# One inference step of a hybrid trunk: every other half linear takes its PSUM bank from the pool of the other products

## The chip, the cores and the metric

The kernel runs on one core of a Trainium2 chip. The metric is the device time of one execution in microseconds (us). The kernel before was timed in three runs: 2755.78, 2758.85 and 2760.88 us, median 2758.85. One execution was profiled; its own time is 2755.11 us and its span, from the first to the last instruction, 2753.0 us. All times below are counted from the start of that span.

## The reference

Two layers with shared weights run over 128 context tokens and 512 latent tokens, with D = 1024. Cut to what the change touches, a layer computes:

```python
h = rms_norm(x, lp['g_pre1']) * (1 + sc1) + sh1
(cb, cc, cx, aq, ak, av, dn_q, dn_k, dn_v, dn_z, dn_beta, dn_a, gate_logits) = jnp.split(h @ lp['w_in'], SPLIT_IDX, axis=-1)
# short convolution, attention and gated DeltaNet give ya, yb, yc
mix = (ga * ya + gb * yb + gc * yc) @ lp['w_o']
x = x + gt1 * rms_norm(mix, lp['g_post1'])
h2 = rms_norm(x, lp['g_pre2']) * (1 + sc2) + sh2
ffn = (jax.nn.silu(h2 @ lp['w_gate']) * (h2 @ lp['w_up'])) @ lp['w_down']
x = x + gt2 * rms_norm(ffn, lp['g_post2'])
```

So at the end of each half of a layer there is a seam: a linear (`w_o` or `w_down`), a norm of its result over all 1024 channels, the residual sum, a second norm over all channels, and then the first linears that read it.

## The kernel before

The activations stand transposed: channels on the 128 partitions, the 640 tokens along the free axis, eight tiles for 1024 channels. The tokens are cut into two halves of 320 columns, called half 0 and half 1. Every weight and activation is split into a high and a low part, and a product is three matmuls (L365, L366, L367: high by high, high by low, low by high). A linear of one block of 128 outputs over 1024 inputs is thus 8 x 3 = 24 matmuls of 128x320 for each half, added up in one PSUM bank.

PSUM has two pools of banks in this kernel. `lbank` (L71) gives the tag `l`, three buffers; it serves the linears alone. `bank` (L74) gives the tag `c`, five buffers; it serves everything else: transposes, attention, DeltaNet, the modulation, and the sums of squares of the norms, where a matmul with a matrix of ones (L157) adds up the channels.

Most linears are written by `linear`, which runs both halves of one weight block together. Near a seam another form is used, in which half 1 runs behind half 0: `group` (L412) and the end of `lin_res` (L465) first run all their blocks for half 0 with `lin_half` (L386), then all for half 1. `lin_res` does so for its last six blocks of `w_o` and `w_down`, `group` for the first linears of the next stage (five in the feed-forward; in a layer's start five, one of them the small `wg` linear, which takes its bank itself).

What is written at a seam, in the order of the program text: six half linears of half 0; then `norm(0)`, which sums the squares (tile `ln`), multiplies and adds the residual (L175 and on), squares and adds up the result again and sums it with a second matmul of ones (tile `pn`, in `half_rstd`, L154); then six half linears of half 1, with the pieces of the next norm's application between them; then `norm(1)` with its own `ln` and `pn`; then the half linears of half 0 of the next stage, then those of half 1. The `pn` of a half is therefore written ahead of the half linears that run while it is being worked out.

A scheduler of the language sets the order on each engine when the program is built. It may put an instruction ahead of others that were written earlier, if its operands and its buffer are there. Buffers of one tag are handed out in the order in which the program asks for them. Each engine then works through its own list in that order, and waits on semaphores for the others.

Of the kernel before, what the change touches and what calls it, by code (L numbers as in the profile page):

```python
# [16 lines left out]
HF = NT // 2  # L17
# [35 lines left out]
def tile_trunk(ctx: ExitStack, tc: tile.TileContext, I: dict, O: list, layers=DEPTH):  # L53
# [17 lines left out]
    def lbank():  # L71
        return pp.tile([P, 512], F32, tag="l", name="l", bufs=NL)

    def bank(name):  # L74
        return pp.tile([P, 512], F32, tag="c", name=name, bufs=NB)
# [4 lines left out]
    def hv(t, h):  # L80
        return t[:, h * HF:(h + 1) * HF]
# [282 lines left out]
    def mm3(out, wh, wl, ah, al, first, last):  # L364
        T.matmul(out, lhsT=wh, rhs=ah, start=first, stop=False)  # L365
        T.matmul(out, lhsT=wh, rhs=al, start=False, stop=False)  # L366
        T.matmul(out, lhsT=wl, rhs=ah, start=False, stop=last)  # L367

    def wblocks(src, nk, keep=None):
# [13 lines left out]
            k += n  # L383
        return out

    def lin_half(blocks, acts, h, ev):  # L386
        pb = lbank()[:, :HF]
        i = 0
        for hi, lo, nk in blocks:
            for j in range(nk):  # L390
                ah, al = acts[i]
                mm3(pb, hi[:, j, :], lo[:, j, :], hv(ah, h), hv(al, h), i == 0, i == len(acts) - 1)
                i += 1
        ev(h, pb)
# [17 lines left out]
    def group(items, side=None):  # L412


        bl = [b if callable(b) or isinstance(b, list) else wblocks(b, len(a), k) for b, a, _, k in items]
        for h in range(2):
            for b, (_, a, ev, _) in zip(bl, items):
                if callable(b):
                    b(h)
                else:  # L420
                    lin_half(b, a, h, ev)
                if h == 0:
                    next(side or iter(()), None)
            drain(side)
# [40 lines left out]
    def lin_res(srcw, acts, ys, gs, keeps, part, after, xe, end=False, side=iter(())):  # L465
# [39 lines left out]
        for h in range(2):  # L505
            for i, b in enumerate(bl):
                lin_half(b, acts, h, ev(n0 + i))
                next(side, None)
            drain(side)
            side = norm(h)  # L510
            next(side, None)
# [914 lines left out]
```

## Time and profile before

| what | value |
| --- | --- |
| median of three runs | 2758.85 us |
| profiled execution, own time | 2755.11 us |
| its span | 2753.0 us |
| PE (TensorE matmuls) busy | 2692.1 us, 98% |
| DVE (VectorE) busy | 1564.1 us, 57% |
| ACT (ScalarE) busy | 1256.7 us, 46% |
| mean granted TensorE clock | 0.994 |
| chain that ended last | PE 84%, DVE 7%, DMA 4%, ACT 3% |

Busy time is the sum of what the engine's instructions took, overlaps counted once. PE's matmuls are pipelined: a 128x320 matmul is shown with some 0.31 us, but the next one starts about 0.147 us behind it. The time between starts is therefore the one to count with. In a timeline row the figures are the start, the length, the engine, line and operation, the tiles as out<-in, the shape and the count of equal ones in a row; in brackets stands the idle time of the engine before it and what ended that.

### The profile page before, as it was taken

To read this page: it belongs to the slowest core of one execution; us is meant where nothing else is said; L and a number is where in the kernel's file an instruction comes from. 1 tells how busy PE (TensorE), PEld (TensorE's weight loads), DVE (VectorE), ACT (ScalarE), POOL (GpSimd) and SP (SyncE) were. 2 spreads that over 40 slices of the span, in tenths; PEclk is the share of its full clock that TensorE was granted. 3 is DMA by queue.
4 is the path that set the end of the run, shared out by engine and by line. 5 is a ranking of instruction groups with operands and counts; after the bars stand their busy time and mean duration, and the time that the engine had idled before them with its cause. 6 is when DMAs were issued, how large, how long until landed. Compare 5 with 4: busy or idle time off the path is not lost.

```text
span 2753.0 us, 49627 instructions
## 1 busy us (share of the span) xinstructions
PE 2692.1 (98%) x19706; PEld 2576.6 (94%) x19706; DVE 1564.1 (57%) x3385; ACT 1256.7 (46%) x2863; POOL 26.8 (1%) x148
## 2 busy tenths in 40 slices
PE   7999999999999999999999999999999999999998
PEld 3899998999899999999989999999999999999997
DVE  5586575477744744224476875754777465432344
ACT  4533554565534633223455345545655364332343
POOL 0000000000000000000000000000000000000001
PEclk9999999999999999999999999999999999999999
DMA  8542355533464344444533323333223532222241
GB/s 243 79 78 55 79 93 105 93 66 97 156 164 153 128 131 153 129 155 146 169 90 71 75 49 85 95 85 87 71 93 120 135 105 72 78 73 73 77 124 56
DMA packets 387800, 288.15 MB, mean 105 GB/s; under 512 B 18699, under 2 KB 348145, under 8 KB 387569
## 3 DMA queue, kind: packets, MB, share of 16 engines
q1 hardware_dynamic: 387568, 285.00, 39.5%
q8 instruction: 154, 2.52, 0.4%
q14 instruction: 78, 0.63, 0.1%
HBM read 251.86 MB, written 33.07 MB: 103 GB/s over the span
## 4 chain that ended last, share of the span: by engine, by line
PE 84%; DVE 7%; DMA 4%; ACT 3%; issue 1%; SPq 0%; POOL 0%; DVEq 0%; ACTq 0%
PE l L365 23%; PE l L366 23%; PE l L367 23%; PE pm L326 1%; DMA wraw<-in_w_in_dram 1%; DMA wm<-in_w_mod_dram 1%; PE ptT L785 1%; DMA rowb<-gd 1%; PE po L795 1%; PE scan L1083 1%; PE po L797 1%; PE sco L365 1%; PE po L796 1%; DVE Tt L1002 1%; PE scan L1091 1%
## 5 line engine op out<-in xcount | busy, mean ns | idle before, releaser
L94 ACT CAST whi<-wraw 128x512 fp32r<-128x512 f32 (+1 forms) x540 | 332.3, 615 | 840.6 <-PE l L366 796.1
L95 DVE TENSOR_TENSOR wlo<-wraw,whi 128x512 fp32r<-128x512 f32 (+1 forms) x540 | 367.1, 681 | 525.7 <-ACT whi L94 512.6
L365 PE MATMUL l<-hh,whi 128*128 128x320 f32 x1856 | 587.0, 316 | 3.1 <-ACT ccs L449 3.1
L366 PE MATMUL l<-hl,whi 128*128 128x320 f32 x1856 | 579.8, 312 | 0.0
L367 PE MATMUL l<-hh,wlo 128*128 128x320 f32 x1856 | 579.3, 312 | 0.0
L365 PE MATMUL l<-h2h,whi 128*128 128x320 f32 x1248 | 387.4, 310 | 0.0
L366 PE MATMUL l<-h2l,whi 128*128 128x320 f32 x1248 | 385.3, 309 | 0.0
L367 PE MATMUL l<-h2h,wlo 128*128 128x320 f32 x1248 | 385.3, 309 | 0.0
L365 PEld LDWEIGHTS l<-hh,whi 128*128 128x128 f32 x1856 | 349.8, 188 | 6.8 <-ACT ccs L449 3.6
L366 PEld LDWEIGHTS l<-hl,whi 128*128 128x128 f32 x1856 | 349.9, 189 | 1.9
L367 PEld LDWEIGHTS l<-hh,wlo 128*128 128x128 f32 x1856 | 349.7, 188 | 1.0
L365 PEld LDWEIGHTS l<-h2h,whi 128*128 128x128 f32 x1248 | 234.6, 188 | 7.0 <-ACT fs L429 3.1
L366 PEld LDWEIGHTS l<-h2l,whi 128*128 128x128 f32 x1248 | 234.7, 188 | 0.0
L367 PEld LDWEIGHTS l<-h2h,wlo 128*128 128x128 f32 x1248 | 234.6, 188 | 0.0
L365 PE MATMUL l<-ah,whi 128*128 128x320 f32 x544 | 169.0, 311 | 0.0
L366 PE MATMUL l<-al,whi 128*128 128x320 f32 x544 | 168.2, 309 | 0.0
L367 PE MATMUL l<-ah,wlo 128*128 128x320 f32 x544 | 168.0, 309 | 0.0
L365 PE MATMUL l<-rsh,whi 128*128 128x320 f32 x384 | 119.7, 315 | 0.0
L366 PE MATMUL l<-rsl,whi 128*128 128x320 f32 x384 | 118.4, 312 | 0.0
L367 PE MATMUL l<-rsh,wlo 128*128 128x320 f32 x384 | 118.2, 309 | 0.0
L365 PEld LDWEIGHTS l<-ah,whi 128*128 128x128 f32 x544 | 102.2, 188 | 2.2 <-issue 1.3
L367 PEld LDWEIGHTS l<-ah,wlo 128*128 128x128 f32 x544 | 102.3, 188 | 0.0
(428 smaller groups left out, 5299.2 us busy)
## 6 DMA issues: line engine op xcount, KB each, us to landing
wraw<-in_w_in_dram SPq DMA_DIRECT2D x256, 256.0 KB, 4.9
wm<-in_w_mod_dram SPq DMA_DIRECT2D x80, 512.0 KB, 4.7
wraw<-in_w_gate_dram SPq DMA_DIRECT2D x88, 256.0 KB, 2.9
wraw<-in_w_up_dram SPq DMA_DIRECT2D x88, 256.0 KB, 3.3
wraw<-in_w_down_dram SPq DMA_DIRECT2D x80, 256.0 KB, 2.9
mixo<-mixd SPq DMA_DIRECT2D x32, 320.0 KB, 5.9
wm<-in_w_mod_dram SPq DMA_DIRECT2D x32, 256.0 KB, 4.7
wraw<-in_w_pb_dram SPq DMA_DIRECT2D x32, 256.0 KB, 2.8
```

What stands on the lines that cost most here:

```text
L94: A.copy(hi, src)
L95: V.tensor_sub(lo, src, hi.bitcast(F32))
L326: T.matmul(pm[32 * u:32 * u + 2, 0:256], lhsT=sc[:, k, :], rhs=w[:, u * 256:(u + 1) * 256], start=(n == 0), stop=(n == KD - 1))
L365: T.matmul(out, lhsT=wh, rhs=ah, start=first, stop=False)
L366: T.matmul(out, lhsT=wh, rhs=al, start=False, stop=False)
L367: T.matmul(out, lhsT=wl, rhs=ah, start=False, stop=last)
L785: T.transpose(pt[:, i, q * P:(q + 1) * P], sm_[q][:, kt * P:(kt + 1) * P], ident)
L795: T.matmul(po, lhsT=vh, rhs=th, start=(kt == 0), stop=False)
L796: T.matmul(po, lhsT=vl, rhs=th, start=False, stop=False)
L797: T.matmul(po, lhsT=vh, rhs=tl, start=False, stop=(kt == 4))
L1002: V.tensor_add(Tt[:, j + 1:32, 0:j], Tt[:, j + 1:32, 0:j], tv)
L1083: T.matmul(pst[:, 1, :], lhsT=XT[h, d][:, c, :], rhs=r, start=True, stop=True)
```

## The change

`lin_half` keeps a turn that flips with every call. Calls one, three, five and so on take a bank of the tag `l` as before; the others take one of the tag `c`, under the name `lc`. Nothing else is changed: all instructions and their shapes are the same, 18,024 matmuls among them.

```diff
@@ -383,8 +383,12 @@
             k += n
         return out
 
+    turn = [0]
+
     def lin_half(blocks, acts, h, ev):
-        pb = lbank()[:, :HF]
+
+        turn[0] ^= 1
+        pb = (lbank() if turn[0] else bank("lc"))[:, :HF]
         i = 0
         for hi, lo, nk in blocks:
             for j in range(nk):
```

The built order moves on PE at the seams. The first place is the seam of `w_o` in layer 0, half 1, from the sum of squares `ln` to the second sum `pn` (the tiles `l` and `lc` are the first linears of the feed-forward for half 0, `ct` is a transpose). Before:

```order
L157 MATMUL ln_10568<-sqt_10544,ones_66 128x320
L366 MATMUL l_10693<-h2l0_9844,wkh_10637 128x320
...
L365 MATMUL l_10726<-h2h0_9843,wkh_10649 128x320
...
L365 MATMUL l_10757<-h2h0_9843,wkh_10661 128x320
...
L365 MATMUL l_10790<-h2h0_9843,wkh_10673 128x320
...
L366 MATMUL l_10790<-h2l6_9856,wkh_10679 128x320
L157 MATMUL pn_10613<-acc_10590,ones_66 128x320
L261 MATMUL ct_10626<-ident_64,rows_10618 128x128
L367 MATMUL l_10790<-h2h6_9855,wkl_10680 128x320
```

The same place on PE in the changed kernel:

```order
L157 MATMUL ln_10568<-sqt_10544,ones_66 128x320
L367 MATMUL l_10693<-h2h3_9849,wkl_10638 128x320
L367 MATMUL l_10757<-h2h0_9843,wkl_10662 128x320
...
L365 MATMUL l_10821<-h2h0_9843,wk_10683 128x320
...
L367 MATMUL l_10821<-h2h7_9857,wk_10684 128x320
L157 MATMUL pn_10613<-acc_10590,ones_66 128x320
L261 MATMUL ct_10626<-ident_64,rows_10618 128x128
L365 MATMUL lc_10726<-h2h0_9843,wkh_10649 128x320
...
L365 MATMUL lc_10790<-h2h0_9843,wkh_10673 128x320
```

The three products of the tag `l` (10693, 10757, 10821) now stand ahead of `pn`, and both products of the tag `c` (10726, 10790) stand behind it. Between the last `ln` matmul and `pn` there were 91 matmuls, and now there are 59.

The second place is the seam of `w_down` in layer 0, half 1, into the first linears of layer 1 (`wg` is the small linear, `l_16025` the first one of half 1, `bgG` belongs to the DeltaNet gates). Before, on PE:

```order
L157 MATMUL ln_15749<-sqt_15725,ones_66 128x320
L366 MATMUL l_15867<-hl4_15050,wkh_15829 128x320
...
L365 MATMUL l_15929<-hh0_15041,wkh_15847 128x320
...
L825 MATMUL l_15960<-hh0_15041,wg_15811 32x320
...
L365 MATMUL l_15982<-hh0_15041,wk_15857 128x320
...
L157 MATMUL pn_15794<-acc_15771,ones_66 128x320
L836 MATMUL bgG_16150<-cst_65,lg_15818 128x16 x2
...
L365 MATMUL l_16025<-hh0_15041,wkh_15823 128x320
```

The same place on PE in the changed kernel:

```order
L157 MATMUL ln_15749<-sqt_15725,ones_66 128x320
L366 MATMUL l_15867<-hl4_15050,wkh_15829 128x320
L366 MATMUL l_15929<-hl2_15046,wkh_15847 128x320
...
L829 MATMUL l_15960<-hl2_15046,wg_15811 32x320
...
L157 MATMUL pn_15794<-acc_15771,ones_66 128x320
L365 MATMUL lc_15898<-hh0_15041,wkh_15835 128x320
...
L365 MATMUL lc_15982<-hh0_15041,wk_15857 128x320
...
L365 MATMUL l_16025<-hh0_15041,wkh_15823 128x320
```

Here 93 matmuls stood between the last `ln` and `pn`, and now 44 do; the 48 of the two `lc` products come behind `pn` and ahead of half 1.

## Rows read from the trace of the kernel before

**Rows 1.** The page's first part: busy us, share and count of PE.

```profile
PE 2692.1 (98%) x19706; PEld 2576.6 (94%) x19706; DVE 1564.1 (57%) x3385; ACT 1256.7 (46%) x2863; POOL 26.8 (1%) x148
```

**Rows 2.** Timeline of PE at the seam of w_o, layer 0: start, us, engine...

```profile
897.02 0.41 PE L365 MATMUL l<-mh,wkh 128*128 128x320 f32 x1 [1.46 <-ACT y L481]
...
902.71 0.41 PE L365 MATMUL l<-mh,wk 128*128 128x320 f32 x1 [1.35 <-ACT y L481]
...
906.34 0.31 PE L365 MATMUL l<-mh,whi 128*128 128x320 f32 x1
...
909.87 0.70 PE L157 MATMUL ln<-acc,ones 128*128 128x320 f32 x2
...
910.56 0.81 PE L157 MATMUL ln<-sqt,ones 128*128 128x320 f32 x2
910.96 0.55 PE L366 MATMUL l<-h2l,wkh 128*128 128x320 f32 x1
911.35 0.30 PE L367 MATMUL l<-h2h,wkl 128*128 128x320 f32 x1
...
922.74 0.42 PE L365 MATMUL l<-h2h,wkh 128*128 128x320 f32 x1 [0.99 <-DVE fg L431]
...
925.79 0.70 PE L157 MATMUL pn<-acc,ones 128*128 128x320 f32 x2
```

**Rows 3.** Timeline of PE at the seam of w_o, layer 1.

```profile
2247.93 0.41 PE L365 MATMUL l<-mh,wkh 128*128 128x320 f32 x1 [1.45 <-ACT y L481]
...
2253.66 0.41 PE L365 MATMUL l<-mh,wk 128*128 128x320 f32 x1 [1.34 <-ACT y L481]
...
2281.09 0.56 PE L365 MATMUL l<-h2h,wkh 128*128 128x320 f32 x2 [0.57 <-ACT h2h L188]
```

**Rows 4.** Timeline of PE at the seam of w_down, layer 0, half 1.

```profile
1436.93 0.81 PE L157 MATMUL pn<-acc,ones 128*128 128x320 f32 x2 [1.45 <-DVE acc L152]
...
1442.24 0.90 PE L365 MATMUL l<-hh,wkh 128*128 128x320 f32 x2 [4.15 <-ACT hh L188]
```

**Rows 5.** Windows, last ln matmul to pn: stretch, length, busy us (count), clock, DMA.

```profile
884.17:898.16 13.99, 12.53 (x82) 12.11 (x82) 11.97 (x28) 8.20 (x19) 0.00 (x0) 1.00 0.20 56
...
910.56:925.79 15.23, 14.24 (x96) 13.82 (x95) 15.08 (x38) 11.59 (x27) 0.00 (x0) 1.00 0.78 276
1391.69:1405.79 14.10, 14.10 (x95) 13.71 (x94) 12.19 (x30) 7.83 (x17) 0.77 (x10) 1.00 0.11 22
...
1420.70:1436.93 16.23, 14.78 (x112) 12.70 (x111) 14.63 (x35) 9.70 (x26) 0.00 (x0) 0.98 0.78 225
2235.09:2249.07 13.98, 12.53 (x83) 12.04 (x82) 11.97 (x28) 8.16 (x18) 0.00 (x0) 1.00 0.20 56
...
2261.50:2277.62 16.12, 16.12 (x108) 15.78 (x107) 16.08 (x41) 11.15 (x27) 0.00 (x0) 1.00 0.59 211
```

**Rows 6.** Timeline of DVE: the last addition before pn, w_o, half 1, both layers.

```profile
925.01 0.48 DVE L152 TENSOR_TENSOR acc<-acc,sqt 128x320 f32<-128x320 f32 x1
...
2276.76 0.49 DVE L152 TENSOR_TENSOR acc<-acc,sqt 128x320 f32<-128x320 f32 x1
```

**Rows 7.** PE past the opening seams: waits for a bank, layers 0 and 1.

```profile
114.53 0.64 PE L365 MATMUL l<-hh,whi 128*128 128x320 f32 x1 [2.75 <-ACT ccs L449]
114.96 0.47 PE L366 MATMUL l<-hl,whi 128*128 128x320 f32 x1
115.23 0.47 PE L367 MATMUL l<-hh,wlo 128*128 128x320 f32 x1
...
1482.67 0.42 PE L365 MATMUL l<-hh,whi 128*128 128x320 f32 x1 [0.33 <-ACT ccs L449]
```

**Rows 8.** Granted clock behind the wait of 4.15 us, and matmuls in it.

```profile
1438.40:1445.20 6.80, 2.96 (x11) 2.93 (x12) 5.04 (x11) 3.81 (x8) 0.00 (x0) 0.50 0.52 102
...
1443.20 0.47 PE L366 MATMUL l<-hl,wkh 128*128 128x320 f32 x1
1443.47 0.47 PE L367 MATMUL l<-hh,wkl 128*128 128x320 f32 x1
```

## The prediction

> **What bounds the kernel now.** I read the page's busy times first, then the gaps of PE in the timeline, then the seams in windows. The page has PE busy for 2692.1 us of a span of 2753.0 us [rows 1]: the kernel is its matmuls, and a change can win only what PE idles or lose by making it idle more. A half linear of 24 matmuls takes 3.53 us from its first start (906.34) to the next instruction's (909.87 [rows 2]), 0.147 us for each. I take this pace to be the same for a bank of either pool, so what counts is how long PE stands at semaphores.
>
> At the seams of `w_o` PE stands for banks: 1.46, 1.35 and 0.99 us in layer 0 [rows 2], 1.45 and 1.34 us in layer 1 [rows 3]. Each is the first matmul of a half linear that waits for the eviction of the linear three before it (ACT `y`, DVE `fg`): three `l` buffers aren't enough there. Together that is 6.6 us. At the seam of `w_down` in layer 0 PE waits 1.45 us at `pn` for the last addition of squares, and then 4.15 us for the first input of half 1 [rows 4]. At the seam of `w_o` in layer 1 it waits 0.57 us for such an input [rows 3].
>
> The third thing to see is how long a `pn` takes to become ready. From the second `ln` matmul of a half to its `pn` the six stretches last 13.99, 15.23, 14.10, 16.23, 13.98 and 16.12 us [rows 5]. DVE is busy for 11.97 to 16.08 us of them, so this chain (multiply, add the residual, square, add up, eight times) goes at the pace of DVE and ACT and not of PE. That PE could come to `pn` at 925.79 without a gap [rows 2], and be busy for all of 14.10 and 16.12 us in two of the stretches [rows 5], is because its list had enough other matmuls to fill them.
>
> **The change, part by part.** No instruction is added, taken away or resized; 42 half linears change their bank, and the built order moves around them. DVE, ACT and SP move a few rows at the same places, with the same instructions; I cost that at nothing, because what they do there is paced by the same chain, and put its doubt into the range.
>
> *The bank waits that go.* Half linears now rotate over three `l` and up to five `c` buffers. The five waits above are at linears that get a buffer earlier: -6.6 us, and no less than 0.
>
> *The place of `pn`.* The order shows a cost. `pn` itself takes a `c` buffer, and is asked for ahead of the half linears that used to run while it ripened. As an `lc` product gets a `c` buffer only after `pn` has got its own, all `lc` products stand behind `pn` on PE, and only every other product is left ahead of it. PE takes its list in order: at 1436.93 it stood 1.45 us at `pn` [rows 4] with products of the other half behind it. So PE now arrives at `pn` early, and waits there, with the `lc` matmuls queued behind. In the changed order the matmuls between the second `ln` and `pn` are 72 and 59 (`w_o`, layer 0, half 0 and half 1), 68 and 44 (`w_down`, layer 0), 72 and 44 (`w_o`, layer 1). At 0.147 us they take 10.58, 8.67, 10.00, 6.47, 10.58 and 6.47 us. The `ln` itself takes 0.65 us of PE (910.56 to 911.35, less one matmul in between [rows 2]). I take the chain to be as long as before, but to end where `pn` could have begun: the last addition ended at 925.01 + 0.48 = 925.49 and 2276.76 + 0.49 = 2277.25 [rows 6], some 0.25 and 0.32 us ahead of `pn` with the time to start. Chain less matmuls less `ln` gives the new waits:
>
> - `w_o`, layer 0: 13.99 - 10.58 - 0.65 = 2.8, and 15.23 - 0.25 - 8.67 - 0.65 = 5.7 us
> - `w_down`, layer 0: 14.10 - 10.00 - 0.65 = 3.5, and 16.23 - 6.47 - 0.65 = 9.1 us
> - `w_o`, layer 1: 13.98 - 10.58 - 0.65 = 2.8, and 16.12 - 0.32 - 6.47 - 0.65 = 8.7 us
>
> Together +32.4 us. In the seam of `w_down`, layer 1, no second norm follows, no `pn` is asked for, and the order of the matmuls stays: 0.
>
> *What this gives back.* PE has 48 matmuls, 7.1 us, of `lc` products to do behind the `pn` of half 1. So the waits behind it (4.15 us [rows 4], 0.57 us [rows 3]) go, and so does the 1.45 us at `pn`, which is part of the 9.1: -6.2 us. With the bank waits the sum is 32.4 - 6.6 - 6.2 = +19.6 us.
>
> *Next inputs.* The `lc` products of a stage's end are done late and the next stage's first products start in front of the `ln` of half 1, on inputs that come one by one. The nearest row is the 0.57 us [rows 3]. With up to three such waits at each of three seams that is 0 to 5 us, and I take +2, nearer to one at each. Past the opening of layer 1 the wait for a bank of a copy is 0.33 us where layer 0 has 2.75 us [rows 7]; with three `l` buffers in another phase it may be either: 0 to +2.4, I take +1.
>
> *The clock.* Behind the wait of 4.15 us the granted clock stood at 0.50 (1.2 of 2.4 GHz) for 6.8 us [rows 8], and matmuls started 0.27 us apart (1443.20 to 1443.47) up to 1445.2; behind the 2.75 us they also stood 0.27 apart (114.96 to 115.23 [rows 7]). The wait of 1.46 us does no such thing: its stretch, 884.17 to 898.16, is at 1.00 [rows 5]. Some 3 us at half pace after a wait, with 11 matmuls 0.12 us late each, are 1.3 us. Four new waits are longer than 2.75 us, so 5.3 us, less the 1.3 us that goes with the 4.15: +4 us. It is 0 if none falls, and 8 if the two waits of 2.8 us count too and the stretches are longer. On this the Trainium skill, "TensorE: Matmul & The Clock Gate", in "HAM oscillation — how this bites in real kernels", says that idle gaps of PE bring it back to half rate and that each following burst pays again. The trace agrees behind 2.75 and 4.15 us, and not behind 1.46; applied to all six new waits it would make +6.5 us of the +4.
>
> **Sum.** 19.6 + 2 + 1 + 4 = +26.6 us. On the profiled execution's own 2755.1 us that is 2781.7 us. That execution is 3.7 us below the median of the runs, from which it would be 2785.5 us. I forecast 2784 us, about 0.9% slower.
>
> **Rivals.**
>
> *Only the bank waits go (faster).* If `pn` were ready when PE reaches it, nothing would replace the five waits: 2755.1 - 6.6 = 2748.5 us, 2752 from the median. For it: all five rows name an eviction [rows 2, 3]. It decides from the point where the chains take no more than what PE now has ahead of `pn`: 11.2, 9.3, 10.7, 7.1, 11.2 and 7.1 us. Against it: they last 14 to 16 us, and in 910.56 to 925.79 DVE worked for 15.08 of 15.23 us [rows 5]. I give it 4%. The Trainium skill, "Perfetto Trace Analysis", in "Optimizing Tensor Performance", "Matmuls", has independent groups rotate through different PSUM banks, so that an eviction lies beside the next group's matmuls. By that rule alone this rival would be the result; the bank waits of the trace agree with it, and it doesn't look at who else asks for those banks.
>
> *The chain gets shorter.* While PE stands, it hands DVE and ACT fewer evictions. In 910.56 to 925.79 DVE had 38 instructions of about 0.4 us [rows 5]; two of the four products of the feed-forward move behind `pn`, with two DVE operations for each half. 4 x 0.48 us = 1.9 us less at two seams, and up to 1 us at the other four, give some 8 us. Without any cost of the clock this ends at 2755.1 + 26.6 - 8 - 4 = 2770 us. For it: DVE is full there. Against it: the work of the norm alone, eight times five operations, is most of it, and no row tells how the rest is ordered now. 17%.
>
> *The clock falls often and for longer.* Each of the six waits, and those for next inputs, is followed by up to 6.8 us at half pace, as the longest stretch of rows 8: 6 x 2 us more than I count, 2796 us. For it: the new waits are longer than any in the middle of the trace. Against it: of the 6.8 us only 3 lay behind the wait's end. 14%.
>
> *It changes nothing.* The waits at `pn` merely replace those for banks and inputs, as at the first half of `w_o` (2.8 us against 1.46 + 1.35): 2755 to 2764. It needs the second halves to be as even as the first. 5%.
>
> **How the numbers follow.** The forecast, with its own range of 2775 to 2792, has 60%. The range to hold the time 8 times in 10 takes in the shorter chain and part of the frequent clock: 2768 to 2797. A measurement of this kernel can tell about 0.2%, 5.5 us, from no change. Faster by more: the first rival, 0.04. Within: part of the last one, 0.04. Slower by more: 0.92.
>
> **What would show it.** In the new trace `pn` (L157) should carry idle time of PE with DVE's `acc` as what ended it, six times, the largest at the second halves of `w_down` in layer 0 and `w_o` in layer 1, 8 to 9 us each; the 4.15 us for `hh` should be gone, and no wait for `y` or `fg` stand at the seams. The granted clock should show 0.50 behind the long ones. The order moves little elsewhere, so the stretches between seams should keep their length within 1 us. I am wrong if `pn` has no gap, if its gaps are half of these (the chain followed PE), or if another place, such as the weights' loads, grows.

## The result, and the profile after

The changed kernel takes 2784.78 us (median of six runs, 2782.98 to 2794.24), the kernel before 2757.98 us (six runs, 2755.68 to 2761.3): 1.0099 of its time, with an interval of 1.0087 to 1.011. The profiled execution took 2783.01 us, with a span of 2780.9 us and a mean granted clock of 0.991.

The page's first part, to set against [rows 1]:

```profile
PE 2700.5 (97%) x19706; PEld 2582.9 (93%) x19706; DVE 1567.2 (56%) x3385; ACT 1259.9 (45%) x2863; POOL 26.9 (1%) x148
```

The instructions and their counts are the same. PE's busy time grew by 8.4 us and the span by 27.9 us, so most of the loss is PE standing still. The view of waits on PE says for what: engine, line, releaser, then us in total, how often, and the longest.

```profile
PE pn L157 <- DVE acc L152: 29.3, 6, 8.4
...
PE l L365 <- ACT ccs L453: 4.5, 2, 2.7
...
PE l L365 <- ACT hh L183: 2.8, 2, 1.5
...
PE l L365 <- ACT h2h L183: 0.2, 1, 0.2
```

One row carries the result: six waits at `pn`, 29.3 us together, where there had been one of 1.45 us [rows 4]. In the kernel before, the same view has 5.6 us for `y`, 1.0 us for `fg` and 4.1 us for the late `hh` of L188 [rows 2 to 4]; none of the three is in it now.

PE's timeline at the seam of `w_o` in layer 0, to set against [rows 2]:

```profile
886.69 0.81 PE L157 MATMUL ln<-sqt,ones 128*128 128x320 f32 x2
...
900.67 0.78 PE L157 MATMUL pn<-acc,ones 128*128 128x320 f32 x2 [2.61 <-DVE acc L152]
...
916.21 0.70 PE L157 MATMUL ln<-sqt,ones 128*128 128x320 f32 x2
...
931.01 1.43 PE L157 MATMUL pn<-acc,ones 128*128 128x320 f32 x2 [5.30 <-DVE acc L152]
...
932.31 0.61 PE L365 MATMUL lc<-h2h,wkh 128*128 128x320 f32 x1
932.72 0.47 PE L366 MATMUL lc<-h2l,wkh 128*128 128x320 f32 x1
932.99 0.47 PE L367 MATMUL lc<-h2h,wkl 128*128 128x320 f32 x1
...
936.36 0.31 PE L365 MATMUL lc<-h2h,wkh 128*128 128x320 f32 x1
936.51 0.31 PE L366 MATMUL lc<-h2l,wkh 128*128 128x320 f32 x1
```

The reader is to see two things. From the second `ln` to `pn` it is 13.98 us (886.69 to 900.67) and 14.80 us (916.21 to 931.01), for 13.99 and 15.23 us before [rows 5], where the 15.23 hold 0.25 us in which `pn` could already have begun [rows 6]: the chain hardly changed. And the `lc` products start right behind `pn`, at 932.31, though they read the same `h2` as the `l` products that ran long before: they had nothing to wait for but their place in PE's list. The Trainium skill, "PSUM — Partial Sum Buffer", "Engine vs sequencer instructions", says that matmuls start and complete in program order; these rows agree. At first the `lc` matmuls start 0.27 us apart, and from 936.36 on 0.15 us, the pace of [rows 2].

The same view at the seam of `w_down` in layer 0, to set against [rows 4]:

```profile
1402.37 0.81 PE L157 MATMUL ln<-sqt,ones 128*128 128x320 f32 x2
...
1416.57 0.78 PE L157 MATMUL pn<-acc,ones 128*128 128x320 f32 x2 [3.43 <-DVE acc L152]
...
1432.28 0.56 PE L365 MATMUL l<-hh,wkh 128*128 128x320 f32 x2 [1.52 <-ACT hh L183]
...
1434.90 0.78 PE L157 MATMUL ln<-sqt,ones 128*128 128x320 f32 x2
...
1436.69 0.31 PE L366 MATMUL l<-hl,wkh 128*128 128x320 f32 x1
1436.84 0.31 PE L367 MATMUL l<-hh,wkl 128*128 128x320 f32 x1
1437.08 0.73 PE L829 MATMUL l<-hh,wg 128*32 128x320 f32 x2
1437.90 0.56 PE L365 MATMUL l<-hh,wkh 128*128 128x320 f32 x2
...
1451.60 1.44 PE L157 MATMUL pn<-acc,ones 128*128 128x320 f32 x2 [7.09 <-DVE acc L152]
```

Both `pn` wait, 3.43 and 7.09 us, where only the second did, for 1.45 us; behind it the 4.15 us for `hh` are gone.

The same view at the seam of `w_o` in layer 1, to set against [rows 3]:

```profile
2254.91 0.81 PE L157 MATMUL ln<-sqt,ones 128*128 128x320 f32 x2
...
2268.79 0.81 PE L157 MATMUL pn<-acc,ones 128*128 128x320 f32 x2 [2.49 <-DVE acc L152]
...
2285.45 0.74 PE L157 MATMUL ln<-sqt,ones 128*128 128x320 f32 x2
...
2301.10 0.90 PE L157 MATMUL pn<-acc,ones 128*128 128x320 f32 x1 [8.36 <-DVE acc L152]
```

Again the first half waits little and the second much (2.49 and 8.36 us); the waits for `y` of [rows 3] are gone.

The granted clock, in windows of the changed kernel (stretch, length, busy us and count of PE, PEld, DVE, ACT, POOL, clock, DMA share, GB/s):

```profile
117.00:120.40 3.40, 2.05 (x14) 2.05 (x15) 1.43 (x2) 2.13 (x6) 0.00 (x0) 1.00 0.49 117
902.10:905.50 3.40, 3.40 (x15) 3.40 (x14) 1.92 (x5) 1.94 (x4) 0.00 (x0) 0.50 0.26 77
929.40:936.20 6.80, 5.19 (x18) 4.69 (x19) 5.70 (x12) 3.08 (x9) 0.00 (x0) 0.50 0.39 115
1417.50:1420.90 3.40, 3.40 (x14) 3.40 (x14) 1.01 (x3) 2.25 (x5) 0.00 (x0) 0.50 0.27 77
1448.20:1455.10 6.90, 3.50 (x11) 3.11 (x12) 3.79 (x9) 2.32 (x5) 0.00 (x0) 0.51 0.75 287
1502.80:1506.30 3.50, 3.50 (x15) 3.50 (x14) 3.42 (x8) 0.69 (x2) 0.00 (x0) 0.51 0.48 111
2269.00:2273.00 4.00, 4.00 (x27) 3.84 (x27) 1.86 (x5) 2.42 (x5) 0.00 (x0) 1.00 0.23 67
2294.70:2304.90 10.20, 3.80 (x12) 3.41 (x13) 7.57 (x19) 5.24 (x13) 0.00 (x0) 0.50 0.36 141
```

At a clock of 0.50, TensorE ran at 1.2 of 2.4 GHz. It did so behind or around five of the six waits at `pn`, and not behind that of 2.49 us (2269.00 to 2273.00). For each matmul of a linear in such a stretch, from the first `kk` (a product of the DeltaNet, early in a layer) to the last norm, I take the time since the start ahead of it, less idle time, less 0.147 us. These add up to 9.0 us, and to 4.3 us in the kernel before: +4.7 us. The matmuls of `pn` itself aren't in this sum; with all matmuls in it the difference is some +7 us.

The two waits for a bank of a copy past the opening of each layer, to set against [rows 7]:

```profile
118.35 0.41 PE L365 MATMUL l<-hh,whi 128*128 128x320 f32 x1 [2.72 <-ACT ccs L453]
...
1501.45 0.41 PE L365 MATMUL l<-hh,whi 128*128 128x320 f32 x1 [1.76 <-ACT ccs L453]
```

**Where the time went.** I cut each trace at PE's starts. A seam of `w_o` runs from the first `ln` to the first full linear behind the group (`h2h` by `wlo`, L367), the seam of `w_down` from its first `ln` to the first `kk` of layer 1; in the changed kernel these are 886.00 to 959.08, 1401.12 to 1487.36 and 2254.22 to 2328.48. All in us; the median is that of the runs.

| kernel | w_o, layer 0 | w_down, layer 0 | w_o, layer 1 | rest of the span | median |
| --- | --- | --- | --- | --- | --- |
| before | 64.98 | 80.46 | 65.22 | 2542.3 | 2757.98 |
| after | 73.08 | 86.24 | 74.26 | 2547.3 | 2784.78 |
| e1_linres | 65.78 | 83.96 | 70.47 | 2542.2 | 2767.55 |
| e2_group | 69.13 | 81.64 | 70.34 | 2551.9 | 2770.43 |
| e3_late | 65.26 | 79.65 | 65.17 | 2543.4 | 2754.76 |
| e5_pn_l | 90.77 | 104.91 | 92.45 | 2548.8 | 2840.94 |
| e6_flip | 78.20 | 87.57 | 79.10 | 2546.3 | 2798.23 |
| e7_nb4 | 64.75 | 80.69 | 65.14 | 2561.5 | 2776.95 |
| e8_own | 66.76 | 81.55 | 67.71 | 2562.5 | 2782.70 |
| e4_nl4 | 62.15 | 80.91 | 61.97 | 2565.8 | 2774.79 |

Of the 27.9 us, 22.9 lie in the three seams (8.1, 5.8 and 9.0) and 5.0 in the rest. Of these 5.0, the start up to the first `kk` has 3.9 (103.32 us against 99.46 us). In the eight kernels below the start took 98.9 to 104.2 us, in no order that their edits would explain, so I don't put it down to the change.

### The profile page after: what moved, and what is told of

It reads as the page before. It is cut to its first block, busy times and chain, and to the rows that moved or that the text cites. A ratio compares the mean times of both kernels' runs of the same rounds, so it can differ in the third digit from the quotient of the medians.

```text
span 2780.9 us, 49627 instructions
## 1 busy us (share of the span) xinstructions
PE 2700.5 (97%) x19706; PEld 2582.9 (93%) x19706; DVE 1567.2 (56%) x3385; ACT 1259.9 (45%) x2863; POOL 26.9 (1%) x148
## 3 DMA queue, kind: packets, MB, share of 16 engines
q8 instruction: 154, 2.52, 0.4%
## 4 chain that ended last, share of the span: by engine, by line
PE 85%; DVE 7%; DMA 4%; ACT 2%; issue 1%; SPq 1%; POOL 0%; DVEq 0%; ACTq 0%; POOLq 0%
PE l L365 22%; PE l L366 22%; PE l L367 22%; PE lc L365 1%; PE lc L366 1%; PE lc L367 1%; PE pm L326 1%; DMA rowb<-gd 1%; DMA wraw<-in_w_in_dram 1%; PE ptT L789 1%; DMA wm<-in_w_mod_dram 1%; PE po L799 1%; DVE acc L152 1%; PE scan L1087 1%; PE sco L365 1%
## 5 line engine op out<-in xcount | busy, mean ns | idle before, releaser
L367 PE MATMUL l<-hh,wlo 128*128 128x320 f32 x1856 | 580.1, 313 | 0.0
L367 PE MATMUL l<-h2h,wlo 128*128 128x320 f32 x1248 | 385.3, 309 | 0.0
L367 PEld LDWEIGHTS l<-hh,wlo 128*128 128x128 f32 x1856 | 350.2, 189 | 1.0
L367 PEld LDWEIGHTS l<-h2h,wlo 128*128 128x128 f32 x1248 | 234.6, 188 | 0.0
L365 PE MATMUL l<-ah,whi 128*128 128x320 f32 x512 | 159.1, 311 | 0.0
L366 PE MATMUL l<-al,whi 128*128 128x320 f32 x512 | 158.3, 309 | 0.0
L367 PE MATMUL l<-ah,wlo 128*128 128x320 f32 x512 | 157.9, 308 | 0.0
L367 PE MATMUL l<-rsh,wlo 128*128 128x320 f32 x384 | 118.3, 310 | 0.0
L365 PEld LDWEIGHTS l<-ah,whi 128*128 128x128 f32 x512 | 96.2, 188 | 2.2 <-issue 1.3
L366 PEld LDWEIGHTS l<-al,whi 128*128 128x128 f32 x512 | 96.3, 188 | 0.0
```

## The experiments

My theory I call the queue: `pn` gets its bank of the tag `c` ahead of the `lc` products, these therefore stand behind it on PE, and PE waits at `pn` with ready matmuls behind. One rival I call sharing: the half linears hold banks of `c` that other work needs, and the loss goes with how many do. Another I call the turn: taking two tags by turns, whichever they are, makes the order worse.

Ratios are to the kernel before, run on the same chip. The order of the built program gives the number of matmuls between the last `ln` and `pn`, for `w_o` of layer 0, `w_down`, `w_o` of layer 1, half 0 and half 1 of each (a dash stands where PE didn't wait):

| kernel | matmuls ahead of pn | PE's waits at pn, us |
| --- | --- | --- |
| before | 79, 91, 91, 93, 79, 104 | -, -, -, 1.45, -, - |
| after | 72, 59, 68, 44, 72, 44 | 2.61, 5.30, 3.43, 7.09, 2.49, 8.36 |
| e1_linres | 72, 85, 68, 92, 72, 62 | 2.60, -, 3.43, 1.67, 2.52, - |
| e2_group | 79, 71, 91, 45, 79, 71 | -, 1.88, -, 7.41, -, 4.56 |
| e6_flip | 72, 24, 68, 38, 72, 24 | 2.96, 9.57, 3.21, 6.07, 2.89, 9.57 |

**e1_linres and e2_group: one half of the change each.** The turn flips in the ends of `lin_res` alone, or in `group` alone.

```diff
-    def lin_half(blocks, acts, h, ev):
-        pb = lbank()[:, :HF]
+    turn = [0]
+    def lin_half(blocks, acts, h, ev, swap=False):
+        turn[0] ^= swap
+        pb = (lbank() if turn[0] or not swap else bank("lc"))[:, :HF]
...
-                lin_half(b, acts, h, ev(n0 + i))
+                lin_half(b, acts, h, ev(n0 + i), True)
```

(that is e1_linres; in e2_group the `True` stands in `group`'s call instead)

> Every other half linear takes a bank of tag c in the ends of w_o and w_down alone (24 calls); the first linears of a stage (18 calls) keep tag l. Queue theory (an lc product stands behind the pn that was written ahead of it): the waits at pn of the first halves stay as in the changed kernel, 2.6, 3.4 and 2.5 us, those of the second halves (5.3, 7.1, 8.4) go; four bank waits of w_o go (5.6 us). Sum +3 to +9 us over before: 2761 to 2767. Sharing theory (each lc takes a buffer off the other products, loss by number of calls): 24 of 42 calls, 24/42 x 27 = +15 us: 2773, with the time lost all along.

> The other part alone: tag c in the first linears of a stage (18 calls), tag l in the ends of w_o and w_down. Queue theory: the waits at pn of the second halves stay near 5.3, 7.1 and 8.4 us = 20.8; what they take the place of (1.45 and 4.15 at the opening of layer 1, 0.99 and 0.57) is 7.2; +13.6, and some 3 us at half clock: +13 to +19, 2771 to 2777, no wait at the first halves' pn. Sharing theory: 18/42 x 27 = +12 us: 2770, and less than the other part.

e1_linres took 2767.55 us, 1.0040 (1.0027 to 1.0054); e2_group 2770.43 us, 1.0045 (1.0029 to 1.0061). The view of waits on PE, of e1_linres:

```profile
PE pn L157 <- DVE acc L152: 10.2, 4, 3.4
...
PE l L365 <- DVE fg L435: 5.9, 2, 4.2
```

The same of e2_group, where the four waits for `y` of [rows 2, 3] are still there:

```profile
PE pn L157 <- DVE acc L152: 13.8, 3, 7.4
...
PE l L365 <- ACT y L485: 5.2, 4, 1.5
```

The table above places them. With only `lin_res` changed, new waits stand at the first halves alone, as long as in the full change (2.60, 3.43, 2.52; the 1.67 us were 1.45 before); with only `group` changed, at the second halves alone. Each `pn` waits where the products written behind it have `c` banks, as the queue says. The two times by themselves separate nothing: 2767.55 us lies 0.6 us above the queue's range and 2770.43 us 0.6 us under it, at the time that sharing gave. I missed two things. In e2_group two of the waits are smaller than those of the full change, because more matmuls stayed ahead of `pn`: 71 for 59 and 44; in layer 0 PE also stood 1.64 us ahead of it, at 927.62, for a weight (DVE `wk`). And in e1_linres waits for the eviction `fg` came to 1.69 and 4.24 us, for 0.99 us and none in the kernel before. The rest of the span is also 9.6 us longer in e2_group than in the kernel before; its clock stood at 0.50 near 208, 461 and 1587 us too, where nothing was edited. Its four runs took 2765.84, 2766.62, 2774.25 and 2774.96 us, and the last is the profiled one, so some of the 9.6 us isn't in every execution; what it is stays open.

**e3_late: `c` banks only late in a group.** Twelve half linears take one: the fourth and the sixth of half 1 in `lin_res`, and the fourth of half 0 in `group`.

```diff
-    def lin_half(blocks, acts, h, ev):
-        pb = lbank()[:, :HF]
+    def lin_half(blocks, acts, h, ev, c=False):
+        pb = (bank("lc") if c else lbank())[:, :HF]
...
-                    lin_half(b, a, h, ev)
+                    lin_half(b, a, h, ev, n in ((3,), ())[h])
...
-                lin_half(b, acts, h, ev(n0 + i))
+                lin_half(b, acts, h, ev(n0 + i), h == 1 and i in (3, 5))
```

> Tag c only for half linears that PE reached after pn anyway in the kernel before: the fourth and sixth of half 1 in w_o and w_down, and the fourth of half 0 in the first linears of a stage (12 calls). Queue theory: no wait at pn over 1.5 us, the bank waits of 1.46 and 1.45 us at the fourth product go: 2753 to 2758, same as before or up to 0.2% faster. Sharing theory: 12/42 x 27 = +8 us: 2766.

2754.76 us, 0.9991 (0.9983 to 1.0000): no loss. Waits on PE:

```profile
PE l L365 <- ACT hh L188: 4.9, 1, 4.9
PE pn L157 <- DVE acc L152: 3.3, 3, 1.6
...
PE l L365 <- ACT y L481: 2.9, 2, 1.5
...
PE l L365 <- DVE fg L431: 2.1, 2, 1.1
```

Here 79 to 96 matmuls stay ahead of each `pn`, and it waits 3.3 us in all. Sharing as such costs nothing, then; the place in the list does. Of the waits for banks that for `y` at the fourth product is gone in both layers, and that at the fifth stays (1.46 us in layer 0, 1.35 us before); the waits for `fg` grew from 1.0 to 2.1 us, and the wait for `hh` stands as in the kernel before. This is the best version that I ran, but it gains no more than can be told from nothing.

**e5_pn_l: no half linear in `c`, but `pn` in `l`.** This brings the queue in by the other door.

```diff
-        pr = bank(name)[:, :HF]
+        pr = (lbank() if name == "pn" else bank(name))[:, :HF]
```

> The kernel before (all half linears on tag l), with the bank of pn taken from tag l too. Queue theory: now all products of a seam stand behind pn, none ahead of it, so PE waits at pn for the whole chain less ln, 11 to 15 us six times; +60 to +85 us over before: 2818 to 2843. Sharing theory: pn is six more users of l, a bank wait of 1.5 us each: +9 us: 2767.

2840.94 us, 1.0306 (1.0288 to 1.0325). PE's timeline at the seam of `w_o` in layer 0 (`l<-acc,ones` is what was `pn`):

```profile
889.52 0.81 PE L157 MATMUL ln<-sqt,ones 128*128 128x320 f32 x2
901.97 1.43 PE L157 MATMUL l<-acc,ones 128*128 128x320 f32 x2 [11.65 <-DVE acc L152]
902.74 0.94 PE L365 MATMUL l<-mh,wkh 128*128 128x320 f32 x1
```

Nothing at all is left between `ln` and `pn`, PE waits through the whole chain, and the linears come out behind it. The other five waits are 13.94, 11.66, 13.73, 11.65 and 13.98 us, 76.6 us in all with this one. With no linear in `c` the loss is three times that of the change: sharing can't make it, the queue says it.

**e6_flip: the turn begins with the other tag.** As many `lc` products as in the change, but the first of each stage is one.

```diff
-    turn = [0]
+    turn = [1]
```

> The changed kernel with the turn begun the other way, so that the even calls take tag c. The count of c calls is the same. In the first linears of the feed-forward only two of five products of half 0 stay on tag l: in the built order 24 matmuls stand between ln and pn at the second half of w_o in place of 59 (layer 0) and 44 (layer 1), and 38 in place of 44 at w_down; the first halves keep 72, 68, 72. Queue theory: each matmul less is 0.147 us more of waiting: 5.3 -> 10.4, 7.1 -> 8.0, 8.4 -> 11.3 us, first halves as in the changed kernel; +9 us over the changed kernel, 2790 to 2798. Sharing theory (loss by number of calls): the same 2785.

2798.23 us, 1.0146 (1.0129 to 1.0163), some 13 us above the change and just over the queue's range; by the profiled executions 5.0 us of it are at `pn`. In the view of waits the row of `pn` is

```profile
PE pn L157 <- DVE acc L152: 34.3, 6, 9.6
```

At the second halves of `w_o` only 24 matmuls are left ahead of `pn`, and 9.57 us are waited at each. The same number of banks taken costs more when fewer products stand ahead of `pn`. The waits of the second halves, 9.57, 6.07 and 9.57 us, were below those that I had expected (10.4, 8.0 and 11.3 us), most of all at `w_down`, where the term of the prediction is too large as well (below).

**e7_nb4, e8_own and e4_nl4: what a bank is worth, and `lc` on a tag of its own.** A tag of its own for `lc` needs a bank, which the tag `c` gives up; e7_nb4 is the kernel before with that bank missing, and is what the other two are compared with.

```diff
-NL, NB = 3, 5
+NL, NB = 3, 4
```

(e7_nb4; e4_nl4 is the kernel before with `NL, NB = 4, 4`; e8_own is e7_nb4 and the change, with the line below in place of the changed one)

```diff
-        pb = (lbank() if turn[0] else bank("lc"))[:, :HF]
+        pb = (lbank() if turn[0] else pp.tile([P, 512], F32, tag="lc", name="lc", bufs=1))[:, :HF]
```

> The kernel before with four buffers of tag c in place of five, nothing else; the eighth bank lies idle. It prices a c buffer by itself. Queue theory: the order at the seams is the same, so the seams keep their length (65, 80, 65 us) and no pn waits over 1.5 us; what is lost lies in the stretches between, where attention and the transposes use tag c: 0 to +15 us. Sharing theory: a buffer less at all times must cost more than one borrowed at the seams, so more than the changed kernel's 27 us.

> As the kernel with four c buffers, but every other half linear takes its bank from a tag of its own with one buffer: the products alternate as in the changed kernel, and pn and they no longer ask for the same tag. Queue theory: no wait at pn over 1.5 us at any of the six places; some waits for the single buffer; within -7 to +8 us of the kernel with four c buffers. Turn theory (splitting the products over two tags is enough to bring pn forward, whatever the tag): the waits at pn stay at 2.5 to 8.4 us, 29 us in all, over the kernel with four c buffers.

> The kernel before with the eight banks parted four and four: a fourth buffer for the linears, taken from tag c for good. Queue theory: the bank waits at the seams of w_o (1.46, 1.35, 1.45, 1.34 us) go, pn doesn't wait; the loss of the fifth c buffer is that of the kernel with four c buffers; so 4 to 7 us under that kernel. It beats the kernel before only if a c buffer is worth less than that.

e7_nb4 took 2776.95 us, 1.0069 (1.0054 to 1.0085), 19.7 us above the kernel before by the medians (2757.3 us on that chip): more than the 0 to 15 us of the queue, and less than the 27 us that sharing asked for at the least. Its seams are those of the kernel before within 0.3 us, so with one `c` bank less `pn` isn't hurt. The loss lies ahead of `w_o`, 12.4 us in layer 0 (from the first `kk` to the first `ln`, 796.4 for 784.0 us) and 6.0 us in layer 1. The largest of its new waits on PE are at the attention's `vn`, for the DVE operation `yc` that empties the bank of a transpose, and at `ptT`, for the ACT operation `p` on the scores:

```profile
PE vn L654 <- DVE yc L1157: 5.3, 2, 3.7
...
PE ptT L785 <- ACT p L740: 5.1, 6, 2.8
```

e8_own took 2782.70 us, 1.0093 (1.0076 to 1.0110), 5.8 us above e7_nb4. It takes tags by turns just as the change does, and two rows of its waits on PE are

```profile
PE l L365 <- ACT h2h L183: 4.3, 2, 2.2
...
PE pn L157 <- DVE acc L152: 1.9, 3, 1.4
```

88 to 101 matmuls are back ahead of `pn`, and its 29.3 us are gone. The turn by itself therefore doesn't make these waits; taking turns with the tag that `pn` uses does. What remains of loss against e7_nb4 are 5.4 us in the seams, with waits for inputs among them.

e4_nl4 took 2774.79 us, 1.0065 (1.0049 to 1.0080), 2.2 us under e7_nb4, where I had expected 4 to 7; the runs of the two overlap, so this is no gain that can be told. The seams of `w_o` are 2.6 and 3.2 us shorter, and no wait for `y` or `fg` is left in its trace. So a fourth `l` bank does what the change did to the bank waits, without the cost at `pn` (2.0 us of waits there); but it comes from the tag `c`, where it is worth more, and outside the seams e4_nl4 is 4.3 us longer than e7_nb4.

## Why the prediction was right

I forecast 2784 us and 2781.7 us for the profiled execution's own time; it was 2784.78 and 2783.01 us. Term by term:

| term | predicted, us | measured, us |
| --- | --- | --- |
| bank waits that go | -6.6 | -6.6: none of the five is left |
| six waits at pn | +32.4 | +29.3 |
| given back | -6.2 | -6.2: 4.15 and 0.57 gone, 1.45 now in the six |
| next inputs | +2 | +0.2: 1.52 and 0.24, for 1.55 in five of 0.2 to 0.5 |
| copy's bank | +1 | +1.4: 1.76 for 0.33, and 2.72 for 2.75 |
| clock | +4 | +4.7, the linears' matmuls alone |
| start, not in the prediction | 0 | +3.9 |
| sum | +26.6 | +26.7, of 27.9 in the span |

**The chain stays, PE comes early.** From the second `ln` to `pn` it was to be 13.99, 14.98, 14.10, 16.23, 13.98 and 15.80 us, and was 13.98, 14.80, 14.20, 16.70, 13.88 and 15.65 us. The rival of a shorter chain is thereby out: the evictions that moved behind `pn` did not make DVE and ACT faster through it. With no product left ahead of `pn`, in e5_pn_l, the chain of a first half was 1.5 us shorter (889.52 to 901.97, 12.45 us), so the rival's effect exists, but it did not come with this change. That the place of `pn` is the cause, and not only goes with it, was shown from four sides: `lc` products late in a group don't hurt (e3_late), `pn` in `l` hurts most (e5_pn_l), fewer matmuls ahead of it hurt more (e6_flip), and a tag of its own takes the waits away (e8_own).

**One wait was mis-sized.** At the second half of `w_down` I said 9.1 us, and it was 7.09. The chain was 0.5 us longer. But PE got there at 1451.60 - 7.09 = 1444.51, 9.61 us after the second `ln`, where I had 44 x 0.147 + 0.65 = 7.12 us. The 44 aren't all of the pace of [rows 2]: 16 of them are the small `wg` matmuls, for which the trace has 32 records, and each tile of `hh` was used as it came: from 1437.08 to 1437.90 it is 0.82 us for one pair of `wg` records. What I should have added to this term is 2.5 us. The other five were up to 0.4 us shorter than said. Idle time counts from the shown end of the matmul ahead, some 0.16 us later than the start at which the next one could have come (0.31 against 0.147 us), which my difference left out.

**The clock and the rest.** +4.7 for +4 us looks close, but it isn't so by the rule that I used. The wait of 2.61 us cost half pace and that of 2.49 us did not, and 1.4 us came behind the wait of 1.76 us for `ccs`, which I had not counted. The new wait of 3.43 us at `w_down` cost next to nothing by it, as the kernel before had been at half pace there too (1417.90 to 1421.30, rows at the end of this text), which I had overlooked. And the sum leaves out `pn` itself: at half pace it took 1.50 us from its start to the second matmul of the linear behind it (1451.60 to 1453.10), where it took 0.76 us at full pace (900.67 to 901.43). With all matmuls counted the term is some +7 us, and too small in the prediction. The stretches between seams were to keep their length within 1 us. From `w_o` to `w_down` they did (442.04 for 441.98 us in layer 0, 408.15 for 408.32 us in layer 1). From the first `kk` to `w_o` they did not: 782.68 for 784.02 us in layer 0, 766.85 for 763.50 us in layer 1, where the wait for `ccs` and the half pace behind it are 2.9 of the 3.4 us. Some 2 us of the seams' 22.9 are in no term of the table; `pn` at half pace, which the clock's term leaves out, is about as much. That the time came out so near is in part luck: the start's 3.9 us made up for what `pn` and the inputs had too much in my sum, and without it the profiled execution would have lost 24, not 28 us.

## What to carry to other kernels

A buffer pool is also an order. If an instruction that waits long takes its buffer from a pool, whatever draws on the same pool behind it is likely to stand behind it on an in-order engine too, ready or not; so, before moving work to a pool with spare buffers, look for who else asks there, and count how much work stays ahead of the one that waits. Moving only products that run behind that instruction anyway cost nothing here, and gained nothing that could be told.

## What the runs showed of the hardware

The length of a wait alone didn't tell whether the clock would fall. In one and the same trace it stood at 0.50 behind idle times of 2.61 us (902.10 to 905.50) and 1.76 us (1502.80 to 1506.30), and at 1.00 behind 2.72 us (117.00 to 120.40) and 2.49 us (2269.00 to 2273.00). The 2.72 us are the wait for `ccs` that lasted 2.75 us in the kernel before, with half pace behind it [rows 7]. The Trainium skill, "TensorE: Matmul & The Clock Gate", "HAM oscillation — how this bites in real kernels", has idle gaps bring the clock down; the trace agrees behind 3.43, 5.30, 7.09 and 8.36 us, and below 3 us it went either way.

Nor did it take one long wait. In the kernel before, at the seam of `w_down` in layer 0, the clock stood at 0.50 behind three waits of under half a microsecond each (PE's timeline, then the window):

```profile
1415.48 0.41 PE L365 MATMUL l<-hh,wkh 128*128 128x320 f32 x1 [0.43 <-ACT hh L183]
1416.35 0.42 PE L366 MATMUL l<-hl,wkh 128*128 128x320 f32 x1 [0.45 <-DVE hl L184]
...
1417.15 0.41 PE L365 MATMUL l<-hh,wkh 128*128 128x320 f32 x1 [0.24 <-ACT hh L183]
...
1417.90:1421.30 3.40, 3.40 (x13) 3.01 (x12) 3.27 (x8) 2.75 (x7) 0.00 (x0) 0.50 0.15 27
```

The fifth bank of the tag `c` was worth 19.7 us to this kernel, and a fourth bank of the tag `l` about 3 us in each seam of `w_o` (2.2 us in the whole time, which can't be told from nothing). The Trainium skill, "Perfetto Trace Analysis", "Matmul Optimizations", asks for all eight PSUM banks to be used; all kernels here but e7_nb4 use eight, and between 2754.76 and 2840.94 us it was who draws on which of them that made the difference.
